# Moving 72 table stores and 8 merged-block stores of a hybrid S5 / SGU mixer layer from SyncE's DMA queue to GpSimd's

## The chip, the cores and the metric

The kernel runs on one core of one Trainium2 chip. The time is the device time of one execution in microseconds (us); lower is better. Three runs of the kernel before gave 746.2, 746.9 and 746.96 us, so its median is 746.9 us.

## The reference

One layer works on 1024 latent tokens of width 1024 and on 256 context tokens. After a layer norm and a modulation, one projection gives seven streams; two branches are computed from them, merged by sigmoid gates, projected out, and added to the input before a last layer norm.

```python
h = _layer_norm(x) * (1.0 + scale) + shift
ua, za, ub, vb, zb, ga, gb = _split_proj(h @ w_in + b_in)
y_a = s5_bidirectional(ua, state from the context)        # 32 groups of 16 channels, 64 states
ya = gelu(y_a) * sigmoid(gelu(y_a) @ glu_w + glu_b) * silu(za)
v = _layer_norm(gelu(vb)) * ln_g + ln_b
vm = einsum('gnm,bkmgc->bkngc', w_s, v in chunks of 128) + b_s
yb = gelu(ub) * vm * silu(zb)
m = sigmoid(ga) * (ya @ w_a) + sigmoid(gb) * (yb @ w_b)
x = _layer_norm(ALPHA * x + gate * (m @ w_o + b_o)) * ln_g + ln_b
```

## The kernel before

All work is float32. A product of two float32 matrices is made of three matmuls (lines 77 to 79): each weight block is loaded as `r_...`, ScalarE (ACT) rounds it to a high part `h_...` (line 72) and VectorE (DVE) subtracts to get the low part `l_...` (line 73). TensorE (PE) then multiplies high by high, low by high and high by low.

The layer norm input is transposed once, and the projection then runs block by block of 128 output channels: `blk0` to `blk3` (the u stream of the gating branch), four pieces `vb0` to `vb3` (the v stream, rows of tokens, into eight PSUM banks `pvb0` to `pvb7`, lines 691 to 699), `blk4` to `blk7` (its z stream, results `zt`), then the gates, `blk20` on. One block is 48 matmuls of 128x512. PE holds the same order of blocks throughout.

The v stream is finished in lines 700 to 708: for each of eight groups of 128 tokens DVE adds a bias out of the PSUM bank (`vt`, line 705), ACT applies gelu (line 706), DVE takes the statistics (`lv0s`, `lv0m`, lines 176 to 182), GpSimd (POOL) computes the inverse square root by a power on a 128x1 column (line 183, tile `lv0m` to `lv7m`), DVE makes the bias (line 188), ACT applies both (line 189). The chunk products `ps` of the gating unit (line 731) read all eight normalised tiles; the small product `prs` (line 719) stands ahead of them.

The state space branch is a convolution. Between about 160 and 220 us DVE makes, for four blocks b of channels and two directions, tables `kca` (lines 512 to 514), which are stored to DRAM as `cad` (line 630). PE turns them into kernels `pk` (lines 646 and 648), evacuated as `wk` (lines 652 to 657). Each `wk` is written to DRAM by eight stores `wd` (line 659), and eight DRAM-to-DRAM copies per block then expand `wd` into the Toeplitz table `mtd` (line 662). `cad` and `mtd` are read back much later (lines 780 and 783, from 400 us on). A scan over the chunk states (lines 608 to 612, three small DVE instructions a step) runs from 190 us; its first 49 steps (`scan(1, 50)`, line 682) are written ahead of the v stream.

The products of the second branch, `mb` (line 840), are stored to DRAM as `md` (line 842), one per gate block, and read back for the merge (line 896).

Every DMA goes through one helper, which issues it on SyncE (SP):

```python
    def dma(o, i):
        nc.sync.dma_start(o, i)
```

The order on each engine isn't the order of the source: a scheduler places every instruction when the program is built, from dependences, buffers and its own estimates, and each engine then works strictly down its own list. A DMA queue is such a list too. So a change of the queue can change the order on ACT, DVE and PE. Buffers come from pools by tag: `RAW` (3 buffers) holds loaded weights, `WSP` (6) their two parts, `ROW` (2) the temporaries of the tables, `G` (27) the large tiles such as `kca` and `zt`, `TMP` (4) evacuations such as `wk`. Of DMA semaphores each queue uses eight in turn, so a DMA waits until the one eight before it has landed.

Of the kernel before, what the change touches and what calls it, by code (L numbers as in the profile page):

```python
# [35 lines left out]
def mixer_kernel(ctx: ExitStack, tc: tile.TileContext, a, out):  # L36
    nc = tc.nc
# [22 lines left out]
    def BANK(name, shape=(128, 512)):  # L60
        return psum.tile(list(shape), F32, name=name, tag="b", bufs=8)

    def dma(o, i):
        nc.sync.dma_start(o, i)

    def row_bcast(name, off, n, nparts=128):
        r = a[name]
        return bass.AP(tensor=r.tensor, offset=r.offset + off, ap=[[0, nparts], [1, n]])
# [18 lines left out]
    def emit_load():  # L87
        key, ap, shape, eng = jobs[emitted[0]]
        emitted[0] += 1
        raw = RAW("r_" + key, shape)  # L90
        dma(raw, ap)
        hi, lo = WSP("h_" + key, shape), WSP("l_" + key, shape)
        split(hi, lo, raw, eng)
        loaded[key] = (hi, lo)
# [28 lines left out]

    cc = C("cc", [128, 8, 2])
    dma(cc, a["cc"])
    wmt = {}

    def load_wm(k):
        for s in range(2):
            wmt[k, s] = WSP(f"wm{k}{s}", (128, 4, 256), F32)  # L130
            dma(wmt[k, s], a["wm"][k, s])
# [362 lines left out]
    for b in range(4):  # L494
        p = BANK(f"pcu{b}")
# [6 lines left out]
    def outer(dst, tmp, eng, pr, xr, xi, b, d, last):  # L502

        gs = slice(32 * d + 8 * b, 32 * d + 8 * b + 8)
        sh = [128, 8, 8, 16]

        def bc(i, x):
            return (pr[:, :, i, gs].rearrange("p k g -> p g k").unsqueeze(3).to_broadcast(sh),
                    x[:, gs, :].unsqueeze(2).to_broadcast(sh))
        p0, x0 = bc(0, xr)  # L510
        p1, x1 = bc(1, xi)
        eng.tensor_tensor(dst, p0, x0, op=OP.mult)
        eng.tensor_tensor(tmp, p1, x1, op=OP.mult)
        eng.tensor_tensor(dst, dst, tmp, op=last)
# [105 lines left out]
    wd = dram.tile([32, 16, 240], F32, name="wd")  # L620
    mtd = dram.tile([4, 128, 8, 128], F32, name="mtd")

    cad = dram.tile([4, 2, 128, 1024], F32, name="cad")
    kca = {}

    def out_powers(b):
        for d in range(2):
            ca = G(f"kca{b}{d}", (128, 8, 8, 16))
            outer(ca, ROW("katmp", (128, 8, 8, 16)), V, pc, xcr, xci, b, d, OP.subtract)
            dma(cad[b, d], ca.rearrange("p g i h -> p (g i h)"))  # L630
            kca[b, d] = ca

    pks = {}
# [1 line left out]
    def kernels(b, d):  # L635
        if d == 0:
            pks[b] = BANK(f"pk{b}", (128, 2, 256))
        pk = pks[b]
        ca = kca[b, d]
        gg = 32 * d + 8 * b  # L640
        for k in range(4):
            for par in range(2):
                lh = bbar[:, gg + 2 * k:gg + 2 * k + 2, :].rearrange("p g h -> p (g h)")
                o = pk[32 * k:32 * k + 32, par, :]
                g = 2 * k + par
                PE.matmul(o[:, 128 * d:128 * d + 112], lh, ca[:, g, d:d + 7, :].rearrange("p i h -> p (i h)"),
                          start=True, stop=True)
                PE.matmul(o[:, 128 * d + 112:128 * d + 128], lh, xcr[:, gg + g, :], start=True, stop=True)
        if d == 0:
            return  # L650
        wk = TMP(f"wk{b}", (128, 2, 240))
        S.activation(wk[:, :, 0:112], pk[:, :, 128:240], AF.Copy)
        S.activation(wk[:, :, 128:240], pk[:, :, 0:112], AF.Copy)
        dm = TMP(f"dm{b}", (128, 3, 16))
        V.tensor_scalar(dm[:, 2, :], mask, cols[:, C_D + b:C_D + b + 1], None, op0=OP.mult)
        V.tensor_tensor(dm[:, 0:2, :], pk[:, :, 112:128], dm[:, 2, :].unsqueeze(1).to_broadcast([128, 2, 16]), op=OP.add)
        V.tensor_tensor(wk[:, :, 112:128], pk[:, :, 240:256], dm[:, 0:2, :], op=OP.add)
        for g in range(8):
            dma(wd[8 * b + g], wk[16 * g:16 * g + 16, g % 2, :])

        for s in range(8):
            dma(mtd[b, 16 * s:16 * s + 16],
                wd[8 * b:8 * b + 8, :, 16 * (7 - s):16 * (7 - s) + 128].rearrange("g h w -> h g w"))

    for i in range(2, 4):
        vm.append(G(f"vm{i}"))
    out_powers(0)
    out_powers(1)

    def kernel_step(b):  # L670
        kernels(b, 0)
        kernels(b, 1)
        if b < 2:
            out_powers(b + 2)
# [80 lines left out]
    def branch(i, g0, w, y, then, mid=None):  # L755

        banks = []

        def evac(p, sl):
            t = TMP("act")  # L760
            S.activation(t, p, AF.Sigmoid, bias=cols[:, C_BLK + g0 + i:C_BLK + g0 + i + 1])  # L761
            banks.append((t, sl))
        proj(g0 + i, evac)
        wh, wl = weights(f"{w}{i // 2}", 0 if g0 + i == GB + 7 else 2)
        if mid is not None:
            mid()
        cs_ = slice(128 * (i % 2), 128 * (i % 2) + 128)
        for t, sl in banks:
            p = BANK(f"pb{g0 + i}")
            for k in range(4):  # L770
                mm3(p, wh[:, k, cs_], wl[:, k, cs_], y[k][0][:, sl], y[k][1][:, sl], k == 0, k == 3)
            then(t, p, sl)
# [4 lines left out]
    def y_tables(b):  # L777
        for d in range(2):
            ca = WSP(f"ca{b}{d}", (128, 8, 8, 16), F32)
            dma(ca.rearrange("p g i h -> p (g i h)"), cad[b, d])  # L780
            cas[b, d] = ca
        mts[b] = RAW(f"mt{b}", (128, 8, 128))
        dma(mts[b], mtd[b])
        ums[b] = ROW(f"um{b}", (128, 8, 128))
        dma(ums[b], ud[b].rearrange("t (h g) c -> (t h) g c", g=8)[:, :, 32:160])

    def y_states(b):
        for d in range(2):
            zt = G(f"z{b}{d}", (128, 8, 128))
            o = 31 if d == 0 else 33  # L790
            for cp in range(2):
                for par in range(2):
                    dst = zt[64 * cp:64 * cp + 64, par:8:2, :]
                    src = vst[64 * par:64 * par + 64, d, o:o + 128, cp, 4 * b:4 * b + 4].rearrange("p c q -> p q c")
                    if par == 0 and cp == 0:
                        S.activation(dst, src, AF.Copy)
                    else:
                        V.tensor_copy(dst, src)
            zs[b, d] = zt
# [35 lines left out]
    md = dram.tile([8, 128, 1024], F32, name="md")  # L835
    for i in range(8):
        mb = G(f"mb{i}")

        def then_b(t, p, sl):
            V.tensor_tensor(mb[:, sl], t, p, op=OP.mult)  # L840
        branch(i, GB, "w_b", yb, then_b, mid=(lambda: y_tables(1)) if i == 7 else None)
        dma(md[i], mb)
        if i == 5:
            y_states(0)
        if i == 6:
            y_tables(0)
# [46 lines left out]
    for i in range(8):  # L893
        m.append(G(f"m{i}"))
        mb = ROW(f"mb{i}", (128, 1024))
# [14 lines left out]
        if i == 4:  # L910
# [3 lines left out]
            for h in range(2):  # L914
                p = BANK(f"pga{h}")
# [141 lines left out]
```

## Time and profile before

| | |
|---|---|
| median of three runs | 746.9 us |
| profiled execution, own time | 750.07 us |
| its span | 748.3 us |
| PE busy | 712.7 us, 95% of the span |
| PE weight loads | 588.0 us, 79% |
| DVE busy | 473.3 us, 63% |
| ACT busy | 237.3 us, 32% |
| POOL busy | 38.3 us, 5% |
| mean granted PE clock | 0.989 of full speed |

The span reaches from the first to the last instruction; the 1.77 us between it and the execution's own time lie around it. DMA issues aren't counted as busy time of an engine; they appear as rows of its queue (SPq, POOLq). Times in the rows are counted from the start of the span. "Idle before" names what ended an engine's idle time.

### The profile page before, as it was taken

Reading aid. Unit: us, or ns where it says so; the run is one execution under the profiler, and the core shown is the slowest. Engines: PE = TensorE matmul, PEld = TensorE weight load, DVE = VectorE, ACT = ScalarE, POOL = GpSimd, SP = SyncE. Lnnn points to the kernel's source line nnn. Section 1 sums busy time; section 2 is a strip of 40 time slices with the busy share of each in tenths; the row PEclk is TensorE's granted clock in tenths of the full one; section 3 lists DMA queues with packets and bytes.
Section 4 is the critical chain, followed back from the end, with each engine's and each line's share of the span. In section 5 each row is a group of like instructions: output and inputs, shape, how many; then the busy total and the mean of one; then the engine's idle time right before and its main releaser. Section 6 shows DMA issues by size and latency. Waiting matters only on the chain.

```text
span 748.3 us, 10063 instructions
## 1 busy us (share of the span) xinstructions
PE 712.7 (95%) x3924; PEld 588.0 (79%) x3924; DVE 473.3 (63%) x1067; ACT 237.3 (32%) x342; POOL 38.3 (5%) x41
## 2 busy tenths in 40 slices
PE   3899999999999699999999999999999999999995
PEld 1656888888887488888888888888888878888885
DVE  4486963559889375898989364223643334492995
ACT  3356846742103613221212265134221211350000
POOL 1010133000001100000000000000000000000221
PEclk9998999999999899999999999999999999999999
DMA  7850273624451211221212493110454223151441
GB/s 307 319 224 29 57 187 116 204 77 155 133 159 44 84 58 56 85 85 57 85 58 84 145 316 130 57 56 29 127 191 132 85 85 112 58 176 50 148 146 72
DMA packets 41295, 89.37 MB, mean 119 GB/s; under 512 B 8352, under 2 KB 21280, under 8 KB 41248
## 3 DMA queue, kind: packets, MB, share of 16 engines
q1 hardware_dynamic: 41248, 88.73, 35.3%
q8 instruction: 31, 0.51, 0.3%
q14 instruction: 16, 0.13, 0.1%
HBM read 73.02 MB, written 17.79 MB: 121 GB/s over the span
## 4 chain that ended last, share of the span: by engine, by line
PE 83%; DVE 10%; ACT 3%; DMA 2%; issue 2%; POOL 1%; SPq 0%; DVEq 0%; POOLq 0%
PE pp L77 13%; PE pp L78 13%; PE pp L79 13%; PE po L952 4%; PE po L951 4%; PE po L953 4%; PE pb L77 4%; PE pb L78 4%; PE pb L79 4%; PE pv L546 2%; DVE scm L608 2%; DVE scs L611 1%; PE py L809 1%; PE pu L77 1%; DVE vst L612 1%
## 5 line engine op out<-in xcount | busy, mean ns | idle before, releaser
L77 PE MATMUL pp<-hh,h_blk 128*128 128x512 f32 x448 | 176.5, 394 | 8.5 <-ACT h_blk L72 6.6
L78 PE MATMUL pp<-hh,l_blk 128*128 128x512 f32 x448 | 175.3, 391 | 0.0
L79 PE MATMUL pp<-hl,h_blk 128*128 128x512 f32 x448 | 174.9, 390 | 0.0
L77 PEld LDWEIGHTS pp<-hh,h_blk 128*128 128x128 f32 x448 | 84.6, 189 | 27.7 <-ACT h_blk L72 7.0
L78 PEld LDWEIGHTS pp<-hh,l_blk 128*128 128x128 f32 x448 | 84.5, 189 | 18.2 <-DVE l_blk L73 0.8
L79 PEld LDWEIGHTS pp<-hl,h_blk 128*128 128x128 f32 x448 | 84.5, 189 | 17.7
L73 DVE TENSOR_TENSOR l_blk<-r_blk,h_blk 128x1024 fp32r<-128x1024 f32 x28 | 34.9, 1248 | 54.3 <-ACT h_blk L72 54.2
L72 ACT ACTIVATE h_blk<-r_blk 128x1024 fp32r<-128x1024 f32 x28 | 29.8, 1068 | 83.1 <-PE pp L78 44.9
L761 ACT ACTIVATE act<-pp,cols 128x512 f32<-128x512 f32 x32 | 21.7, 679 | 100.0 <-PE pp L79 71.6
L608 DVE TENSOR_TENSOR scm<-acat,vst 128x128 f32<-128x128 f32 x158 | 46.1, 292 | 10.1 <-ACT vst L548 5.0
L612 DVE TENSOR_TENSOR vst<-vst,scs 128x64 f32<-128x64 f32 x158 | 35.5, 225 | 5.2
L611 DVE TENSOR_TENSOR scs<-scm 128x64 f32<-128x64 f32 x158 | 35.5, 225 | 4.9
L951 PE MATMUL po<-wobig,mh 128*128 128x512 f32 (+1 forms) x90 | 32.9, 365 | 0.0
L952 PE MATMUL po<-wobig,mh 128*128 128x512 f32 (+1 forms) x90 | 32.9, 365 | 0.0
L953 PE MATMUL po<-wobig,ml 128*128 128x512 f32 (+1 forms) x90 | 32.9, 365 | 0.0
L77 PE MATMUL pu<-hh,uw 128*128 128x512 f32 x64 | 28.5, 451 | 2.5 <-ACT uw L72 1.9
L79 PE MATMUL pu<-hl,uw 128*128 128x512 f32 x64 | 27.0, 424 | 0.9 <-DVE hl L200 0.9
L78 PE MATMUL pu<-hh,uw 128*128 128x512 f32 x64 | 26.9, 421 | 0.0
L698 PE MATMUL pvb<-l_vb,hh 128*128 128x512 f32 x64 | 25.0, 391 | 0.0
L697 PE MATMUL pvb<-h_vb,hh 128*128 128x512 f32 x64 | 25.0, 391 | 0.0
L699 PE MATMUL pvb<-h_vb,hl 128*128 128x512 f32 x64 | 24.9, 389 | 0.0
L79 PE MATMUL pb<-yas,h_w_a 128*128 128x512 f32 x64 | 24.9, 389 | 0.0
(342 smaller groups left out, 1326.7 us busy)
## 6 DMA issues: line engine op xcount, KB each, us to landing
r_blk<-in_w_blk SPq DMA_DIRECT2D x28, 512.0 KB, 3.4
wm<-in_wm SPq DMA_DIRECT2D x16, 512.0 KB, 7.3
x<-in_x SPq DMA_DIRECT2D x8, 512.0 KB, 5.8
cad<-kca SPq DMA_DIRECT2D x8, 512.0 KB, 2.7
md<-mb SPq DMA_DIRECT2D x8, 512.0 KB, 2.6
ca<-cad SPq DMA_DIRECT2D x8, 512.0 KB, 5.6
mb<-md SPq DMA_DIRECT2D x8, 512.0 KB, 4.5
wgt<-in_w_gate SPq DMA_DIRECT2D x8, 512.0 KB, 3.3
```

Of the source, the lines that this page charges most:

```text
L72: first = S.activation(hi, src, AF.Copy)
L73: return first, (eng or V).tensor_tensor(lo, src, hi.bitcast(F32), op=OP.subtract)
L77: PE.matmul(o, wh, rh, start=first, stop=False)
L78: PE.matmul(o, wl, rh, start=False, stop=False)
L79: PE.matmul(o, wh, rl, start=False, stop=last)
L608: V.tensor_tensor(scm, acat.rearrange("p d (o c) q -> p d o (c q)", o=2), both(n - 1, prev).unsqueeze(2).to_broadcast([128, 2, 2, 32]), op ...
L611: V.tensor_tensor(scs4, m4[:, :, 0, :], m4[:, :, 1, :], op=OP.add)
L612: V.tensor_tensor(both(n, 160 if n == 31 else cur), both(n, cur), scs2, op=OP.add)
L697: PE.matmul(pvb[kk], hth[k][:, ks], wh[:, j, :], start=k == 0, stop=False)
L951: PE.matmul(p, mh, wh, start=k == 0, stop=False)
L952: PE.matmul(p, mh, wl, start=False, stop=False)
L953: PE.matmul(p, ml, wh, start=False, stop=k == 7)
```

## The change

A second helper issues on GpSimd, and four kinds of DMA use it: the 8 stores `cad`, the 32 stores `wd`, the 32 expansions `mtd` and the 8 stores `md`. The helper adds four lines above everything that follows, so line 72 of the kernel before is line 76 after, and so on.

```diff
     def dma(o, i):
         nc.sync.dma_start(o, i)
+
+    def dma_side(o, i):
+
+        nc.gpsimd.dma_start(o, i)
...
             outer(ca, ROW("katmp", (128, 8, 8, 16)), V, pc, xcr, xci, b, d, OP.subtract)
-            dma(cad[b, d], ca.rearrange("p g i h -> p (g i h)"))
+            dma_side(cad[b, d], ca.rearrange("p g i h -> p (g i h)"))
...
         for g in range(8):
-            dma(wd[8 * b + g], wk[16 * g:16 * g + 16, g % 2, :])
+            dma_side(wd[8 * b + g], wk[16 * g:16 * g + 16, g % 2, :])
 
         for s in range(8):
-            dma(mtd[b, 16 * s:16 * s + 16],
+            dma_side(mtd[b, 16 * s:16 * s + 16],
                 wd[8 * b:8 * b + 8, :, 16 * (7 - s):16 * (7 - s) + 128].rearrange("g h w -> h g w"))
...
         branch(i, GB, "w_b", yb, then_b, mid=(lambda: y_tables(1)) if i == 7 else None)
-        dma(md[i], mb)
+        dma_side(md[i], mb)
```

The list of POOL in the changed program, from the last of the kernels' stores to the first block store (`lv` are the columns of the v stream's norm):

```order
L68 DMA cad_1577<-kca31_1824 128x1024
L68 DMA mtd_1576<-wd_1575 128x1x128 x8
L68 DMA wd_1575<-wk2_1889 16x240 x8
L68 DMA wd_1575<-wk3_1945 16x240 x4
L68 DMA mtd_1576<-wd_1575 128x1x128 x8
L68 DMA wd_1575<-wk3_1945 16x240 x4
L187 TENSOR_TENSOR lv0m_2348<-lv0m_2348,half_89 128x1
L187 TENSOR_TENSOR lv1m_2358<-lv1m_2358,half_89 128x1
```

```order
L187 TENSOR_TENSOR lv6m_2411<-lv6m_2411,half_89 128x1
L68 DMA mtd_1576<-wd_1575 128x1x128 x8
L187 TENSOR_TENSOR lv7m_2421<-lv7m_2421,half_89 128x1
L68 DMA md_3125<-mb0_3126 128x1024
```

In the program before, the eight `lv` columns follow directly on POOL's table arithmetic. Now 64 DMA issues stand between that arithmetic and `lv0m` (8 `cad`, 32 `wd`, 24 `mtd`), 60 of them from the first `wd` on, and 8 more between `lv6m` and `lv7m`.

The list of ACT before, around the split of weight block `blk5` (`h_blk5`); `vt` and `lv` belong to the v stream, `zt0` is the result of `blk4`:

```order
L189 ACTIVATE vt6_2406<-vt6_2406,lv6m_2411 128x512
L706 ACT_TABLE_LOAD
L706 ACTIVATE vt6_2406<-vt6_2406 128x512
L568 ACT_TABLE_LOAD
L568 ACTIVATE zt0_2427<-pp41_2460,cols_65 128x512
L72 ACTIVATE h_blk5_2291<-r_blk5_2289 128x1024
```

The same place in the changed program:

```order
L76 ACTIVATE h_vb3_2183<-r_vb3_2181 128x1024
L76 ACTIVATE h_blk4_2237<-r_blk4_2235 128x1024
L76 ACTIVATE h_blk5_2291<-r_blk5_2289 128x1024
L710 ACTIVATE vt0_2343<-vt0_2343 128x512 x2
L710 ACTIVATE vt2_2364<-vt2_2364 128x512 x2
L710 ACTIVATE vt4_2385<-vt4_2385 128x512
L76 ACTIVATE h_blk6_2430<-r_blk6_2428 128x1024
```

`h_blk5` stood twenty places behind `h_blk4`: eight gelus and seven norms of the v stream, two results `zt0` and three table loads lay between them; now it stands directly behind `h_blk4`, ahead of all of these. On DVE the biases `vt` and the statistics are likewise interleaved with the last 12 of the 49 scan steps, where they stood behind all of them. PE's list is the same but for one matmul of `blk5`, which moves 23 places back within its block.

## Rows read from the trace of the kernel before

**Rows 1.** The page: busy time by engine; the chain that ended last, by engine.
```profile
PE 712.7 (95%) x3924; PEld 588.0 (79%) x3924; DVE 473.3 (63%) x1067; ACT 237.3 (32%) x342; POOL 38.3 (5%) x41
...
PE 83%; DVE 10%; ACT 3%; DMA 2%; issue 2%; POOL 1%; SPq 0%; DVEq 0%; POOLq 0%
```

**Rows 2.** Timeline of PE, 232 to 258 us: start, us, instruction, [idle before <-releaser].
```profile
233.03 0.39 PE L699 MATMUL pvb<-h_vb,hl 128*128 128x512 f32 x1
235.26 0.47 PE L77 MATMUL pp<-hh,h_blk 128*128 128x512 f32 x1 [1.84 <-DVE vt L705]
...
253.01 1.22 PE L77 MATMUL pp<-hh,h_blk 128*128 128x512 f32 x2 [6.61 <-ACT h_blk L72]
...
257.75 0.39 PE L77 MATMUL pp<-hh,h_blk 128*128 128x512 f32 x1
```

**Rows 3.** Busy time by engine in two stretches; PEclk is the granted clock.
```profile
core 0: us, PE busy (x) PEld busy (x) DVE busy (x) ACT busy (x) POOL busy (x), PEclk, DMA share, GB/s
235.26:246.40 11.14, 11.14 (x48) 8.90 (x48) 10.16 (x34) 9.46 (x14) 3.79 (x7) 1.00 0.01 1
253.01:257.75 4.74, 4.70 (x11) 3.29 (x11) 3.57 (x3) 2.55 (x3) 0.00 (x0) 0.52 0.43 123
```

**Rows 4.** Timeline of ACT, 239 to 253 us.
```profile
239.38 0.80 ACT L189 ACTIVATE vt<-vt,lv0m 128x512 f32<-128x512 f32 x1
...
248.09 1.28 ACT L706 ACT_TABLE_LOAD   x1
...
250.03 1.28 ACT L568 ACT_TABLE_LOAD   x1
...
251.91 1.05 ACT L72 ACTIVATE h_blk<-r_blk 128x1024 fp32r<-128x1024 f32 x1
252.86 0.81 ACT L189 ACTIVATE vt<-vt,lv7m 128x512 f32<-128x512 f32 x1
```

**Rows 5.** Timeline of DVE, 185 to 236 us.
```profile
185.73 1.23 DVE L512 TENSOR_TENSOR kca<-pwf,xc 128x1024 f32<-128x1024 f32 x1 [0.28 <-PE pk L646]
...
188.14 1.22 DVE L514 TENSOR_TENSOR kca<-kca,katmp 128x1024 f32<-128x1024 f32 x1
...
234.43 1.88 DVE L705 TENSOR_TENSOR vt<-pvb,row 128x512 f32<-128x512 f32 x3
```

**Rows 6.** Timeline of SP's DMA queue, 174 to 222 us: start, us, issues.
```profile
174.94 4.93 SPq L64 DMA_DIRECT2D wd<-wk  x8
179.97 0.37 SPq L64 DMA_DIRECT2D cad<-kca  x1
...
181.16 5.13 SPq L64 DMA_DIRECT2D mtd<-wd  x8
...
219.42 1.53 SPq L64 DMA_DIRECT2D r_blk<-in_w_blk  x3
```

**Rows 7.** Timeline of POOL, 115 to 252 us.
```profile
115.40 2.03 POOL L513 TENSOR_TENSOR abtmp<-pb,yb 128x1024 f32<-128x1024 f32 x1 [6.64 <-DMA ud<-uct]
...
238.29 0.55 POOL L183 TENSOR_TENSOR lv0m<-lv0m,half 128x1 f32<-128x1 f32 x1 [106.02 <-DVE lv0m L182]
...
245.35 0.55 POOL L183 TENSOR_TENSOR lv5m<-lv5m,half 128x1 f32<-128x1 f32 x1 [0.34 <-DVE lv6m L181]
245.87 0.55 POOL L183 TENSOR_TENSOR lv6m<-lv6m,half 128x1 f32<-128x1 f32 x1
```

**Rows 8.** DMA issues by line: count, KB each, median us from issue to landing.
```profile
r_blk<-in_w_blk SPq DMA_DIRECT2D x28, 512.0 KB, 3.4
cad<-kca SPq DMA_DIRECT2D x8, 512.0 KB, 2.7
...
mtd<-wd SPq DMA_DIRECT2D x32, 64.0 KB, 2.5
...
wd<-wk SPq DMA_DIRECT2D x32, 15.0 KB, 1.5
```

**Rows 9.** Timeline of PE at 191 us and at 266 us.
```profile
191.09 0.38 PE L646 MATMUL pk<-kca,bbar 128*32 128x112 f32 x2
...
266.50 1.09 PE L719 MATMUL prs<-wst,ones 128*64 128x128 f32 x16
267.43 7.16 PE L731 MATMUL ps<-wst,vt 128*64 128x128 f32 x128
```

**Rows 10.** Timeline of PE, 439 to 448 us.
```profile
439.58 0.46 PE L809 MATMUL py<-ca,z 128*128 128x128 f32 x2 [0.48 <-DMA ca<-cad]
440.86 0.46 PE L809 MATMUL py<-ca,z 128*128 128x128 f32 x2 [0.82 <-DMA ca<-cad]
...
447.36 0.46 PE L807 MATMUL py<-mt,um 128*128 128x128 f32 x2 [0.47 <-DMA um<-ud]
```

## Prediction

> **What bounds the kernel now.** I read the page first: PE is busy for 712.7 of 748.3 us, and the chain that ended last runs through PE for 83%; POOL is busy for 38.3 us only [rows 1]. A change of the stores' queue can therefore gain only where PE waits, and lose only where it makes PE wait longer. So I read PE's timeline through the stretch in which the moved transfers are issued (175 to 270 us) and followed each gap to its releaser. There are two [rows 2]. At 235.26 PE comes out of a gap of 1.84 us: it wants a PSUM bank that DVE empties with `vt`. At 253.01 it comes out of one of 6.61 us: it wants `h_blk5`, the rounded weights of `blk5`. Then the clock. In the stretch 235.26 to 246.40 the granted clock is 1.00, the upper of its two levels, and 48 matmuls take 11.14 us, 0.232 each; from 253.01 to 257.75, behind the gap, it is 0.52, near the lower level, and the ten pitches in it take 4.74 us [rows 3]. At full clock they would take 2.32, so the dip costs 2.42. Together the place costs 1.84 + 6.61 + 2.42 = **10.9 us**.
>
> Why are these two late? DVE's first `vt` is at 234.43 [rows 5], although the last matmul of `pvb` was over at 233.42 [rows 2]: the `vt` stand behind the whole scan in DVE's list. `h_blk5` starts at 251.91, directly behind two table loads of 1.28 us each, at 248.09 and 250.03, and the instructions that need them [rows 4]. Its load wasn't late: the loads issued at 219.42 [rows 6] land 3.4 us later [rows 8], at 222.8, 29 us ahead of the split. It is the order on ACT, not the queue, that holds it.
>
> **The change, part by part.**
>
> *The new order.* In the changed program `h_blk5` stands directly behind `h_blk4`, ahead of the gelus, and the `vt` are mixed with the last twelve scan steps. Both gaps lose their releaser, and the dip behind them its cause: **−10.9 us**. What is late next is the v stream's end, because its norm needs POOL (below). From 260 us on PE's list is the same but for a matmul of `blk5`, and the waits there are under a microsecond each [rows 10], so nothing is known that would take a gain back.
>
> *The issues leave SP.* SP spends 4.93 us on eight `wd`, 5.13 on eight `mtd` and 0.37 on a `cad` [rows 6]. The transfers stay, so only these issue times leave. I cost this at nothing: PE's waits in the stretch aren't for DMAs, and the loads that stood behind the stores get ahead of their need by more than they had.
>
> *The issues come to POOL.* This decides. The inverse square roots of the v stream, `lv0m` to `lv7m`, sit on POOL, 0.55 us each, 0.52 from one to the next [rows 7]. Before, POOL was idle for 106 us ahead of `lv0m` [rows 7]. Now 60 issues stand between the first `wd`, which can start at 174.94 [rows 6] as it did on SP, and `lv0m`; eight more `mtd` stand between `lv6m` and `lv7m`. Behind POOL wait, in this order, DVE (the bias of each norm), ACT (the norm, in order with its weight splits) and PE (`ps`, which reads all eight). Call the mean time of an issue on POOL x. From the power to the norm's start it took 239.38 − 238.29 = 1.09 us [rows 4, 7], the norm takes 0.81 [rows 4]. For waits on landings among the issues I allow 2 us: SP's queue shows 181.16 − 180.34 = 0.82 between a `cad` and the `mtd` behind it [rows 6], and a `wd` lands after 1.5 [rows 8]. So the last norm is done at 174.94 + 2 + 60x + 7 × 0.52 + 8x + 1.09 + 0.81 = 182.5 + 68x.
>
> When does PE need it? Without the gaps `blk4` starts at 233.42; two blocks of 11.14 [rows 3], `prs` 267.43 − 266.50 = 0.93, and 14 of the 128 pitches of `ps` (7.16 / 128 × 14 = 0.78) until the first that reads the last tile [rows 9] give 257.4. So the cover holds for x up to (257.4 − 182.5) / 68 = **1.10 us**; each 0.1 beyond costs 6.8.
>
> The trace of before has no issue on POOL. Bounds: not under SP's own 0.62, 0.64 and 0.37 for the same transfers [rows 6], as no row has any queue issue them faster; not over 2.03, a POOL instruction over 128x1024 elements [rows 7], or 2.5, the time of a whole `mtd` to its landing [rows 8]. Between them I take what stands nearest, the shortest POOL instruction (0.55) and SP's issue together: 1.17 for a `wd`, 1.19 for an `mtd`, 0.92 for a `cad`. That counts the arithmetic of the power as well, so x is somewhat less: **1.1**, just under cover. **Stall: 0.** By the upper end, 2.5, the last norm would be done at 352.5, 95 us late; by the lower, 0.62, at 224.7 with no effect.
>
> The Trainium skill, "DMA: Bandwidth & Descriptors", section "Latency and other measured facts", gives GpSimd's queue about 1 us to the first byte against about 0.6 on the hardware path, and puts the difference down to the issue by software. Taking its 1 us for x as an estimate, the last norm is done at 250.5, under cover, and the sum is the same −10.9; no row here shows POOL's figure, while SP's 0.62 agrees with the other.
>
> *A later landing.* DVE's `kca31` started at 185.73 [rows 5]; now it waits until `cad20` has landed, because that still reads the buffer: 174.94 + 9x + 2.7 [rows 8], which is 187.5 at x = 1.1, 1.8 later. Its last instruction ended at 189.36 [rows 5], 1.73 ahead of PE's `pk` at 191.09 [rows 9]. Cost **+0.1 us** at 1.1, 3.7 at 1.5 (then covered by the greater wait).
>
> *`md`, and the tables read back.* The eight `md` come long after the norms, when POOL has nothing that others wait for. `cad` and `mtd` are read from 400 us on, over 100 us after even a slow queue. Both: 0. The two waits at 439.58 and 440.86 are for reads of `cad`, the one at 447.36 for a read of `um`, 0.48, 0.82 and 0.47 [rows 10]; if fewer entries in SP's queue removed them, 1.8 more would be gained. I take 0, and keep it for the range.
>
> **Sum:** −10.9 + 0.1 = −10.8. The profiled execution took 750.07, 3.2 over the median of 746.9 of the three runs. In its frame 739.3; against the median **736**.
>
> **Rivals.** A measurement of this kernel can tell about 0.2%, 1.5 us, from no change.
>
> *B, slower: POOL's queue becomes the bound.* If an issue takes POOL longer than 1.10, `ps` waits 68 us for each us of it, and the clock falls again behind the gap (2.42). The gain is eaten where 68(x − 1.10) + 2.4 = 10.8, at **x = 1.22**. At 1.5 the last norm is done at 284.5, 27.1 late: −10.8 + 27.1 + 2.4 = +18.7, **765.6**; at 2.03 the delay is 63.1 and the time 802. For it: nothing on POOL in this trace ends under 0.55, a full-width instruction takes 2.03, and the margin is 0.12 over my estimate. Against: the pieces I can add are already more than an issue should contain.
>
> *C, no change that can be measured.* The diff alone shifts issues from one list to another, and if the order on ACT were no help, because `h_blk5` then waits for its weights instead, the gap would stay: 746.9. Against it: those weights were issued at 219.42 and landed at 222.8 [rows 6, 8]. A band of x from 1.20 to 1.25, where gain and stall balance, belongs here too.
>
> By the Trainium skill, same page, section "Issuing engines are not separate DMA queues", all queues end on the same 16 DMA engines and a second issuer saves only its issue time, usually little; by that alone the time would be C's 746.9. The rows agree that the transfers weren't what PE waited for; the gain forecast here comes from the order of instructions, of which the rule doesn't speak.
>
> **How the numbers follow.** x decides. Under 1.10 (full gain) I give 0.43, 1.10 to 1.20 (a part of it) 0.16: faster 0.59. C with its band 0.08. B, beyond 1.25, 0.33. The likeliest is A: 736. Its own range is 734 (the three small waits go as well) to 745. B begins where A ends and is open upwards, so the range for all must reach into it: to **764**, x = 1.48, with some 0.15 above that and 0.05 below **734**.
>
> **What would show it.** Right: in PE's timeline no gap after the last `pvb` matmul and none before `blk5`, granted clock 1.00 through both blocks; POOL's queue rows of eight `wd` or `mtd` at 8.8 us or less; `lv0m` no later than 245, `lv7m` by 255.5; no gap ahead of `ps`. Wrong: issue rows of POOL over 9.8 us for eight, a gap of several us that ends with ACT's norm of `lv7m` ahead of `ps`, and a low clock behind it; or a gap at `blk5` that now ends with its load. A PE wait at `pk` near 191 us that ends with DVE would show the `kca31` term larger than 0.1.

## The result, and the profile after

The changed kernel takes **737.6 us** (median of 4 runs, 737.06 to 737.87) where the kernel before, beside it, took 746.9 (4 runs, 746.2 to 747.66). The ratio is 0.9874, 95% interval 0.9857 to 0.9891: 9.3 us, or 1.3%, faster. The forecast was 736, range 734 to 764.

The page of the changed kernel, busy time by engine, which answers to [rows 1]. Unlike issues on SP, the 80 DMA issues count among POOL's instructions (121 against 41) and as its busy time:

```profile
PE 706.3 (96%) x3924; PEld 585.1 (79%) x3924; DVE 469.7 (64%) x1067; ACT 235.1 (32%) x340; POOL 79.6 (11%) x121
```

PE's timeline from the end of the v stream to `ps`, which answers to [rows 2]; the three pieces are the start of `blk4`, the start of `blk5` and the end of both:

```profile
230.07 0.39 PE L703 MATMUL pvb<-h_vb,hl 128*128 128x512 f32 x1
230.30 0.39 PE L81 MATMUL pp<-hh,h_blk 128*128 128x512 f32 x1
...
240.95 0.39 PE L83 MATMUL pp<-hl,h_blk 128*128 128x512 f32 x1
241.18 0.39 PE L81 MATMUL pp<-hh,h_blk 128*128 128x512 f32 x1
...
252.15 1.09 PE L723 MATMUL prs<-wst,ones 128*64 128x128 f32 x16
253.07 1.37 PE L735 MATMUL ps<-wst,vt 128*64 128x128 f32 x22
```

No row carries an "idle before" any more: both gaps are gone, and `ps` starts 0.92 behind `prs`. The clock of this stretch, which answers to [rows 3]:

```profile
230.30:252.15 21.85, 21.85 (x98) 17.83 (x96) 12.65 (x51) 13.42 (x19) 7.46 (x14) 1.00 0.24 72
```

PE is busy for all 21.85 us, at granted clock 1.00, the upper level. ACT's timeline shows why:

```profile
219.39 1.06 ACT L76 ACTIVATE h_blk<-r_blk 128x1024 fp32r<-128x1024 f32 x1 [9.82 <-PE pvb L702]
...
246.82 0.69 ACT L572 ACTIVATE zt<-pp,cols 128x512 f32<-128x512 f32 x1 [0.74 <-PE pp L83]
247.50 0.82 ACT L193 ACTIVATE vt<-vt,lv7m 128x512 f32<-128x512 f32 x1
```

`h_blk5` is made at 219.39, 21.8 us ahead of `blk5`, where it stood at 251.91 [rows 4]; the last norm is done at 248.32, ahead of the point at 253.84 (253.07 + 0.77) at which `ps` first reads it. POOL's timeline, with the waits among its issues, answers to [rows 6, 7]:

```profile
172.49 3.85 POOL L68 DMA_DIRECT2D wd<-wk  x8 [1.07 <-DVE wk L661]
...
178.24 4.21 POOL L68 DMA_DIRECT2D mtd<-wd  x8 [1.34 <-issue]
...
209.07 2.03 POOL L68 DMA_DIRECT2D wd<-wk  x4
227.66 0.56 POOL L187 TENSOR_TENSOR lv0m<-lv0m,half 128x1 f32<-128x1 f32 x1 [16.55 <-DVE lv1m L185]
...
237.17 4.24 POOL L68 DMA_DIRECT2D mtd<-wd  x8
241.37 0.63 POOL L187 TENSOR_TENSOR lv7m<-lv7m,half 128x1 f32<-128x1 f32 x1
```

Eight `wd` take 3.85 us and eight `mtd` 4.21, against SP's 4.93 and 5.13 [rows 6]. POOL is through with these 60 issues (the first is at 172.49) at 211.1 and then idle for 16.55 us until DVE has statistics.

Where did the 9.3 us come from? The two profiled executions differ ahead of the change too: the first matmul of `pk` starts at 167.72 before and at 164.76 after (over all kernels of this study it lies between 162.57 and 168.02, whatever the change). This is about the 3.2 us by which before's profile stood over its median. So I compare lengths of stages, from the start of `pk` on:

| stage, us | before | after | difference |
|---|---|---|---|
| start of `pk` to start of `prs` | 98.78 | 87.39 | −11.39 |
| start of `prs` to the first `py` | 160.47 | 160.46 | 0 |
| first `py` to the last matmul's end | 313.79 | 313.39 | −0.40 |
| last output store issued to the span's end | 4.12 | 6.69 | +2.57 |

These add up to −9.2, within 0.1 of the medians' difference. The last line was not in the forecast. The rows behind it, SP's timeline at the end of the span, before (span 748.3):

```profile
744.18 0.99 SPq L64 DMA_DIRECT2D out<-r  x2
```

and after (span 736.1):

```profile
729.41 0.99 SPq L64 DMA_DIRECT2D out<-r  x2
```

The row holds the last two output stores; the stretch counts from its start. The work ahead of it is the same in both. I call this stretch **the end** below, and the first line of the table **the stage**.

### The profile page after: what moved, and what is told of

Its sections match the earlier page's. It is cut to its first block, busy times and chain, and to the rows that moved or that the text cites. A ratio compares the mean times of both kernels' runs of the same rounds, so it can differ in the third digit from the quotient of the medians.

```text
span 736.1 us, 10107 instructions
## 1 busy us (share of the span) xinstructions
PE 706.3 (96%) x3924; PEld 585.1 (79%) x3924; DVE 469.7 (64%) x1067; ACT 235.1 (32%) x340; POOL 79.6 (11%) x121
## 4 chain that ended last, share of the span: by engine, by line
PE 90%; DVE 4%; DMA 2%; ACT 2%; issue 1%; SPq 0%; POOL 0%; DVEq 0%; POOLq 0%
PE pp L81 14%; PE pp L82 14%; PE pp L83 14%; PE po L957 4%; PE po L955 4%; PE po L956 4%; PE pb L82 4%; PE pb L81 4%; PE pb L83 4%; PE pv L550 3%; PE pvb L701 2%; PE pvb L702 2%; PE pvb L703 2%; PE py L813 1%; PE pu L81 1%; PE pm L210 1%
## 5 line engine op out<-in xcount | busy, mean ns | idle before, releaser
L765 ACT ACTIVATE act<-pp,cols 128x512 f32<-128x512 f32 x32 | 21.8, 682 | 100.5 <-PE pp L83 76.5
L187 POOL TENSOR_TENSOR lo0m<-lo0m,half 128x1 f32<-128x1 f32 x1 | 1.5, 1533 | 266.7 <-DVE lo0m L186 266.7
L81 PE MATMUL pu<-hh,uw 128*128 128x512 f32 x64 | 27.4, 433 | 2.5 <-ACT uw L76 1.9
L82 PE MATMUL pu<-hh,uw 128*128 128x512 f32 x64 | 26.2, 409 | 0.0
```

The source lines that it names most:

```text
L81: PE.matmul(o, wh, rh, start=first, stop=False)
L82: PE.matmul(o, wl, rh, start=False, stop=False)
```

## Experiments

All twelve, with the medians of their own runs; the kernel before gave 746.45 beside e1 to e4, 746.91 beside e5 to e8, 747.73 beside e9 to e12. So kernels of different groups are compared by their ratios, or by stage and end, which come from their profiled executions.

| kernel | us | ratio to before (95%) | stage | end | DMAs on GpSimd |
|---|---|---|---|---|---|
| the changed kernel | 737.6 | 0.9874 (0.9857 to 0.9891) | 87.39 | 6.69 | 80 |
| e1_order_on_sp | 735.55 | 0.9853 (0.9839 to 0.9866) | 87.38 | 4.14 | 0 |
| e2_h_blk5_late | 743.67 | 0.9966 (0.9954 to 0.9979) | 94.10 | 6.47 | 80 |
| e3_one_store | 747.44 | 1.0016 (1.0005 to 1.0027) | 98.25 | 4.29 | 1 |
| e4_act_queue | 755.24 | 1.0114 (1.01 to 1.0128) | 107.35 | 4.11 | 0 |
| e5_md_only | 746.65 | 0.9999 (0.9982 to 1.0016) | 99.42 | 4.0 | 8 |
| e6_tables_only | 737.32 | 0.9867 (0.9849 to 0.9885) | 87.39 | 6.07 | 72 |
| e7_48_more | 747.65 | 1.0009 (0.9996 to 1.0023) | 87.39 | 10.6 | 128 |
| e8_96_more | 757.0 | 1.0132 (1.0116 to 1.0148) | 87.39 | 4.67 | 176 |
| e9_48_more_dve | 741.34 | 0.9914 (0.9895 to 0.9933) | 87.39 | 10.58 | 128 |
| e10_act_order_only | 738.8 | 0.9878 (0.9858 to 0.9899) | 91.12 | 4.11 | 0 |
| e11_mtd_only | 735.78 | 0.9851 (0.9826 to 0.9875) | 87.39 | 4.0 | 32 |
| e12_change_again | 737.79 | 0.9873 (0.9849 to 0.9897) | 87.39 | 6.7 | 80 |

### Is it the order or the queue? e1, e2

**e1_order_on_sp** is the kernel before with every store on SP. Edges that order instructions on one engine, without a wait, impose the changed kernel's order (`heads` holds the instructions: g gelu, n norm, z `zt`, v `vt`, s scan step).

```diff
+    def behind(later, earlier):
+        tc.add_manual_dep(later.ins, earlier.ins.name, mybir.DependencyInfo(
+            mybir.DependencyClass.NoSync, mybir.DependencyReason.DATA), reason="order")
...
+    row = "blk4 blk5 g0 g1 g2 g3 g4 blk6 g5 g6 g7 z40 n0 n1 n2 n3 n4 n5 n6 z4512 blk7 z50 n7 z5512".split()
+    row2 = [("v1", "s41"), ("v3", "s42"), ("v5", "s44"), ("v6", "s45"), ("v7", "s46")]
+    for e, l in list(zip(row, row[1:])) + row2:
+        behind(heads[l], heads[e])
```

> All stores stay on SP as in the kernel before; only the order is taken from the changed kernel: on ACT h_blk5 stands directly behind h_blk4 and the gelus, norms and zt results follow in the changed kernel's order, on DVE the eight vt stand among the scan steps 40 to 46. Theory (the order is the whole gain, the queue has no part in it): the two gaps and the dip go, 10.9 us, and the 2.6 us that the changed kernel's end became longer (from the last output store to the end of the span 6.7 us against 4.1) do not come: 735 to 736 us, 1.5 to 2.5 under the changed kernel's 737.6. Rival (SP's queue is relieved of its stores, so that loads come earlier): nothing is relieved here, 745 to 748 us, with a gap before blk5 that ends with its load.

Measured 735.55, as the theory had it. SP's timeline and ACT's:

```profile
211.61 5.05 SPq L64 DMA_DIRECT2D mtd<-wd  x8
216.70 1.53 SPq L64 DMA_DIRECT2D r_blk<-in_w_blk  x3
```
```profile
221.16 1.06 ACT L78 ACTIVATE h_blk<-r_blk 128x1024 fp32r<-128x1024 f32 x1 [11.64 <-DVE scs L617]
```

The loads of `blk5` and its followers still stand behind the last `mtd`, `h_blk5` is 1.8 us later than in the changed kernel, and it makes no difference: the stage is 87.38 long. The queue has no part in this stage's gain; the order is all of it. The 2 us by which e1 is under the changed kernel are the end: 4.14 against 6.69.

**e2_h_blk5_late** is the changed kernel with one edge more, `h_blk5` behind the second half of `zt0`:

```diff
+            if blk == ZB and sl.start:
+                behind(heads["blk5"], ev)
```

> The changed kernel with its stores on GpSimd, but h_blk5 is held behind zt0's second half on ACT, as it stood before the change. Theory (order): the gap before blk5 and the clock dip behind it come back in good part, 3 to 7 us of gap and 1 to 2.5 us of dip: 742 to 747 us; the gap of 1.84 us at blk4 stays away. Rival (relief of SP's queue): 737 to 738.5 us, no gap of over 1 us before blk5.

Measured 743.67, within the theory's range. ACT's and PE's timelines, and the clock behind the gap:

```profile
243.58 0.67 ACT L578 ACTIVATE zt<-pp,cols 128x512 f32<-128x512 f32 x1
244.15 2.94 ACT L82 ACTIVATE h_blk<-r_blk 128x1024 fp32r<-128x1024 f32 x3
```
```profile
245.24 1.22 PE L87 MATMUL pp<-hh,h_blk 128*128 128x512 f32 x2 [4.64 <-ACT h_blk L82]
```
```profile
245.24:250.00 4.76, 4.72 (x13) 3.36 (x14) 3.48 (x3) 1.84 (x2) 0.00 (x0) 0.65 0.52 151
```

With SP as relieved as in the changed kernel, the gap before `blk5` is back (4.64 us), its releaser is ACT's `h_blk` again, and the clock behind it is 0.65. The stage is 6.71 longer than in the changed kernel. The relief of SP does not help where the order is not there.

### The two gaps apart: e10

**e10_act_order_only** has e1's list `row` for ACT and not `row2` for DVE.

> All stores on SP; only ACT's order is taken from the changed kernel, on DVE the vt stay behind the whole scan. Theory (two separate terms): the gap at blk5 and the dip go (9.0 us), the gap of 1.84 us at blk4 stays: 736.9 to 738.2 us, 1.4 to 2.5 over e1_order_on_sp. Rival (the vt on DVE are what lets h_blk5 pay): 742 us or more.

Measured 738.8, a little over the range. PE's timeline and the clock behind the gap:

```profile
231.64 0.57 PE L83 MATMUL pp<-hh,h_blk 128*128 128x512 f32 x1 [1.85 <-DVE vt L711]
```
```profile
231.64:235.60 3.96, 3.96 (x11) 3.12 (x11) 3.96 (x8) 3.96 (x7) 0.00 (x0) 0.57 0.02 4
```

The gap at `blk4` is there to the hundredth, 1.85 against 1.84 [rows 2], but here the granted clock falls to 0.57 behind it, where it stayed at 1.00 in the kernel before [rows 3]. So the stage is 3.74 longer than e1's, where gap and the 0.16 by which matmuls overlap make 2.0; the dip costs the other 1.7 (ten pitches take 3.96 us, against 2.27 at full clock). In the traces ACT's order alone is worth 98.78 − 91.12 = 7.7 us, DVE's on top of it 3.7.

The dip doesn't need ACT's new order. It stands behind the same gap in e3 below, whose order on ACT is that of the kernel before:

```profile
232.69 0.47 PE L81 MATMUL pp<-hh,h_blk 128*128 128x512 f32 x1 [1.85 <-DVE vt L709]
```
```profile
232.69:236.87 4.18, 4.17 (x11) 3.27 (x12) 4.09 (x11) 2.93 (x6) 0.56 (x1) 0.59 0.02 4
```

In e3 it lengthens nothing, because the wait for `h_blk5` behind it is shorter by as much (5.01 us instead of 6.61). In e5, with the same gap (1.86), the clock stays at 1.00. Why it falls in one execution and not in another is not shown. Without the dip the two orders would be worth about 9.4 and 2.0 us, an estimate from 7.7 + 1.7 and 3.7 − 1.7, close to the 9.0 and 1.84 that were expected.

### Which of the stores turn the order: e5, e6, e11, e12

**e5_md_only** moves `md` alone, **e6_tables_only** all but `md`, **e11_mtd_only** the expansions alone; **e12_change_again** is the changed kernel beside e11.

```diff
-            dma(mtd[b, 16 * s:16 * s + 16],
+            dma_side(mtd[b, 16 * s:16 * s + 16],
```

> Only the eight block stores md go on GpSimd's queue; cad, wd and mtd stay on SP, and ACT's order is that of before. Theory (order): the gaps at blk4 and blk5 stay, nothing is gained. For the end (4.1 us before, 6.7 after the change, 4.3 with a single store on GpSimd): if it grows with the eight semaphores that a queue uses in turn, it is 6.4 to 6.8 us here and the time 748.5 to 749.5; if it grows with the number of stores, it is under 4.6 us and the time 746.5 to 747.5. Rival for the gain (it comes from the md stores leaving SP): under 745.

> The 72 stores and expansions of the tables on GpSimd, the eight md stay on SP; ACT's order is that of the changed kernel. Theory (order): all of the gain, 736.5 to 738.5 us, with an end of 6.4 to 6.8 us if it goes by semaphores or by number of stores. If the longer end belongs to md (late stores), it is 4.1 us and the time 735 us.

> Only the 32 expansions mtd go on GpSimd; ACT's order flips as in the changed kernel, with h_blk5 directly behind h_blk4. Theory (order; the end grows with the number of DMAs on GpSimd, nothing at 8 and 2 us at 72): the same gain ahead of the end, an end of 4.1 to 5.2 us, 735 to 736.5 us. Rival (all the stores must leave SP): 740 us or more.

> The changed kernel again, beside the others on one chip: 737 to 738.5 us, 1 to 3 over e11_mtd_only if the end goes by the number of DMAs, the same as it if not.

Measured 746.65, 737.32, 735.78 and 737.79. `md` gains nothing and costs nothing: both gaps stay (1.86 and 6.60 us on PE), the end is 4.0. The 32 expansions alone bring the whole stage down to 87.39, and with them gone `h_blk5` stands directly behind `h_blk4`, as ACT's timeline in e11 has it:

```profile
209.50 1.06 ACT L76 ACTIVATE h_blk<-r_blk 128x1024 fp32r<-128x1024 f32 x1 [9.82 <-PE pvb L702]
220.38 1.06 ACT L76 ACTIVATE h_blk<-r_blk 128x1024 fp32r<-128x1024 f32 x1 [9.82 <-PE pvb L702]
```

The last eight of them stood directly ahead of `blk5`'s load in SP's list, as e1's rows above show; that the scheduler reckoned this load late because of them is read from the order, not shown apart. e11 is 2.0 under the changed kernel on the same chip; the difference is the end, 4.0 against 6.7. Of the two forecasts for e5's end, the one by number of stores held.

### ACT as the issuer: e4

**e4_act_queue** is the change with `nc.scalar.dma_start` in the helper.

```diff
-        nc.gpsimd.dma_start(o, i)
+        nc.scalar.dma_start(o, i)
```

> The same 80 stores and expansions, issued on ACT instead of GpSimd. The order there has h_blk5 two places behind h_blk4, ahead of the gelus. Theory (order; end lengthened only by GpSimd's queue): the gap before blk5 goes and the end stays 4.1 us; against that stand 72 issues of about 0.6 us on ACT, 43 us between 165 and 230 us, with waits for landings among them, so PE may wait for h_vb2 or h_vb3: 735 us where it does not, up to 745 where it does. Rival (GpSimd's queue itself is needed): 746 us or more with the gap before blk5 as before.

Measured 755.24: ten over what the theory allowed, and yet without the rival's sign, the gap before `blk5`. ACT's timeline and PE's:

```profile
202.38 5.08 ACTq L68 DMA_DIRECT2D mtd<-wd  x8
207.51 0.36 ACT L656 ACTIVATE wk<-pk 128x224 f32<-128x224 f32 x1 [5.15 <-DMA mtd<-wd]
```
```profile
220.32 0.77 PE L701 MATMUL pvb<-h_vb,hh 128*128 128x512 f32 x1 [14.88 <-DVE vst L616]
```

A new gap of 14.88 us stands in the v stream, released by DVE, a little after ACT's evacuations have waited behind eight issues. The theory looked for a late weight split on ACT. That split comes directly behind the evacuations and is done at 209.56 (208.48 + 1.08), 10.8 us before the gap ends; DVE, busy with scan steps until then, makes the low part of these weights only at 221.07:

```profile
221.07 1.22 DVE L77 TENSOR_TENSOR l_vb<-r_vb,h_vb 128x1024 fp32r<-128x1024 f32 x1
```

So what came last came from DVE; why it was late there is not shown. The end is 4.11: it is GpSimd's queue that lengthens it, not the leaving of SP.

### How much POOL can carry: e7, e9, e8

**e7_48_more** and **e8_96_more** add expansions of the last table into a tile `mtx` that nothing reads, ahead of `lv0m`, and hold ACT's order by e1's list; the last two biases of the norms are also held ahead of `blk7`'s split on DVE. The diff shows e7; e8 has 12 in place of 6.

```diff
+        for j in range(6 if b == 3 else 0):
+            for s in range(8):
+                heads["extra"] = nc.gpsimd.dma_start(
+                    mtx[j, 16 * s:16 * s + 16],
+                    wd[24:32, :, 16 * (7 - s):16 * (7 - s) + 128].rearrange("g h w -> h g w"))
```

> The changed kernel with 48 more expansions of the last table on GpSimd's queue (into a DRAM tile that nothing reads), all ahead of lv0m, and the changed kernel's order held on ACT. At 0.53 us an issue they take 25 us: lv0m moves from 227.7 to about 242 us, lv7m to about 246, the last norm still before 249; PE needs it at about 254. Theory (POOL's queue has cover until then): no gap ahead of ps, 737 to 739 us. Rival (issues on POOL cost others time directly, by the DMA engines or by waits behind them): 741 us or more.

Measured 747.65: a miss. ACT's timeline and PE's:

```profile
257.59 0.81 ACT L201 ACTIVATE vt<-vt,lv0m 128x512 f32<-128x512 f32 x1 [14.95 <-DVE lv1m L200]
```
```profile
258.46 0.44 PE L752 MATMUL ps<-wst,vt 128*64 128x128 f32 x4 [2.20 <-ACT vt L201]
```

POOL had `lv0m` at 245.62, but on DVE the biases stood behind four instructions that wait for `prs`:

```profile
256.30 1.13 DVE L742 SCALAR_TENSOR_TENSOR row<-prs,cols,row 128x128 f32<-128x128 f32 x4 [11.60 <-PE prs L740]
```

The scheduler presumably put them there because it counted POOL late; that is not shown. From `prs` to `py` it took 166.43 us, 6.0 more than the changed kernel's 160.46, and the end is 3.9 longer: together the 10 us. **e9_48_more_dve** adds one edge against that:

```diff
+    behind(heads["sg0"], heads["b7"])
```

> As e7_48_more, but on DVE the eight biases of the norms stand ahead of the four instructions that wait for prs; in e7 they stood behind them, which held the norms until 257.6 us whatever POOL did. Theory (POOL's queue has cover until about 254 us): no gap of over 0.5 us ahead of ps; with the end of e7 (10.6 us against the changed kernel's 6.7), if that goes by the number of DMAs, 740.5 to 742.5 us. Rival (the queue costs time even under cover): a gap of 2 us or more ahead of ps and 745 us or more.

Measured 741.34. POOL's, ACT's and PE's timelines:

```profile
242.45 0.74 POOL L193 TENSOR_TENSOR lv0m<-lv0m,half 128x1 f32<-128x1 f32 x1
...
246.10 0.66 POOL L193 TENSOR_TENSOR lv7m<-lv7m,half 128x1 f32<-128x1 f32 x1
```
```profile
250.52 0.81 ACT L201 ACTIVATE vt<-vt,lv7m 128x512 f32<-128x512 f32 x1
```
```profile
252.91 1.26 PE L753 MATMUL ps<-wst,vt 128*64 128x128 f32 x20
```

`lv0m` is 14.8 us later than in the changed kernel and nobody waits: from `prs` to `py` 160.55. All that e9 costs is its end, 10.58.

In the expectation of **e8_96_more**, "the same" is e7:

> The same with 96 more expansions, 50 us of issues: lv0m at about 267 us, the last norm at 272 to 276, PE needs it at about 254. Theory (past its cover POOL's queue is the bound, as in the slower case of the prediction): a gap of 18 to 23 us ahead of ps that ends with ACT's norm, a low clock behind it worth about 2.4 us: 756 to 763 us. Rival (the norms are not what PE waits for): under 745 us.

Measured 757.0. POOL's timeline, PE's, and the clock behind the gap:

```profile
249.44 20.77 POOL L679 DMA_DIRECT2D mtx<-wd  x40 [2.33 <-issue]
269.92 0.87 POOL L193 TENSOR_TENSOR lv0m<-lv0m,half 128x1 f32<-128x1 f32 x1
```
```profile
271.94 9.32 PE L752 MATMUL ps<-wst,vt 128*64 128x128 f32 x95 [18.25 <-ACT vt L201]
```
```profile
271.94:281.00 9.06, 9.01 (x95) 7.42 (x97) 3.65 (x10) 8.50 (x12) 2.42 (x5) 0.62 0.13 36
```

Past its cover POOL's queue is the bound, by the chain that the prediction's slower rival named: POOL, DVE, ACT's norm, `ps`, and a low clock behind it. From `prs` to `py` it took 182.86, 22.4 more than in the changed kernel: the gap of 18.25 and 4.1 behind it.

### The end: e3

**e3_one_store** moves the first `cad` alone.

```diff
-            dma(cad[b, d], ca.rearrange("p g i h -> p (g i h)"))
+            (dma_side if (b, d) == (0, 0) else dma)(cad[b, d], ca.rearrange("p g i h -> p (g i h)"))
```

> The kernel before with one store alone, the first cad at about 168 us, on GpSimd's queue; the order on ACT is that of before. Theory (the mere use of GpSimd's queue lengthens the end of the program): the stretch from the issue of the last output store to the end of the span is 6.5 to 7 us instead of 4.1, the gaps at blk4 and blk5 stay: 749 to 750 us. Rival (the longer end comes from how many or how late GpSimd's stores are): 746 to 747.5 us, end 4.1 us.

Measured 747.44, and the end 4.29: the theory that the mere use of the queue lengthens the end falls. The 1 us by which its median lies over before's is not explained by its trace, whose stage is 0.5 shorter than before's and whose end is 0.17 longer. The DMA engines' busy tenths over the last 7 us of the span, changed kernel:

```profile
DMA  0000003999999940000000000000000000000000
```

and the kernel before:

```profile
DMA  0000000000000000000006999999910000000000
```

In the changed kernel the last transfer is over after 15 of 40 slices, and the rest, 4.4 us against some 1.6 before, shows no transfer and no counted instruction on any engine. An uncounted one stands there in the trace: a DRAIN on GpSimd. It starts with POOL's last power, 1.9 us ahead of the last output stores, and the closing steps of all engines follow when it is over. Before it runs from 742.29 for 1.01 us; in the changed kernel from 727.52 for 7.58 us, to 735.10, and the span ends at 736.1. Over all kernels it goes by the number of DMAs on GpSimd:

| DMAs on GpSimd | 0 | 1 | 8 | 32 | 72 | 80 | 128 | 176 |
|---|---|---|---|---|---|---|---|---|
| DRAIN, us | 1.01 to 1.09 | 1.11 | 1.69 | 3.66 | 6.93 | 7.58 | 11.50 | 5.53 |
| end, us | 4.11 to 4.14 | 4.29 | 4.0 | 4.0 | 6.07 | 6.47 to 6.7 | 10.6 | 4.67 |

Up to 128 that is 0.08 us for each DMA, for the 512 KB stores of e5 as for the 64 KB copies of e11 ((7.58 − 1.01) / 80 and (11.50 − 1.01) / 128 both give 0.082), long after the transfers have landed. The end grows only when the DRAIN outlasts the landing of the last stores. By these numbers that begins near 48 DMAs (an estimate: a DRAIN of 1.9 + 4.1 − 1.0 = 5.0 us). That is why e3, e5 and e11 have the end of the kernel before. At 176 the DRAIN is as long as after 55 DMAs; e8's POOL paused for 2.33 us directly behind its 128th issue (the row at 249.44 above). What GpSimd does for each DMA in the DRAIN, and in that pause, is not shown.

## Why the prediction was right, and where it was off

**What bounds the kernel, and the new order: right.** The two gaps and the dip were forecast to go for −10.9. The stage lost 11.39. Each gap is larger by the 0.16 with which matmuls overlap in the rows (0.39 long, 0.23 apart), 0.3 for both; `blk5` itself got 2.52 shorter (13.49 from its first matmul to `prs` before, 10.97 after) instead of 2.42, and `blk4` 0.1. e1 and e2 show that the order is the cause, from both sides.

Two readings behind the sum were looser than it. Not all of the 2.42 is clock: behind the gap PE's weight loads wait for `l_blk5` too, which DVE makes from the late `h_blk5`. The kernel before, PE's weight loads:

```profile
254.27 0.29 PEld L78 LDWEIGHTS pp<-hh,l_blk 128*128 128x128 f32 x1 [0.76 <-DVE l_blk L73]
```

That is about 0.6 of the 2.42, an estimate: the first three pitches take 1.85 us there (253.01 to 254.86), and 1.28 in e10 at the low clock. The new order removes this wait with the gap, so the sum holds. And e10 and e3 show that a gap of 1.85 us can bring a dip that the trace of the kernel before doesn't have.

**The issues leave SP, costed at nothing: right.** e1 keeps them all on SP and has the same stage. To that extent the Trainium skill's rule, "DMA: Bandwidth & Descriptors", section "Issuing engines are not separate DMA queues", agrees with the runs. By the rule alone the time would have stayed, as in rival C; it did not, because the change of queue came with another order.

**The issues come to POOL: right in sign, the size of the term was off.** The step "I take what stands nearest ... 1.1" took about twice the measured cost. POOL's groups by line, 165 to 245 us:

```profile
L68 POOL DMA_DIRECT2D mtd<-wd x32 | 16.9, 564 | 5.1 <-DMA wd<-wk 3.8 <-issue 1.3
L68 POOL DMA_DIRECT2D wd<-wk x32 | 15.7, 525 | 3.0 <-DMA cad<-kca 1.9 <-DVE wk L661 1.1
L68 POOL DMA_DIRECT2D cad<-kca x6 | 3.4, 562 | 7.2 <-DVE kca L518 4.0 <-DVE dm L660 1.9 <-DMA wd<-wk 1.3
```

An issue takes 0.53 to 0.56 us, below SP's 0.62 and 0.64 for `wd` and `mtd`, which the prediction had set as the lower bound: no row showed a faster queue, and that is no reason why there should be none. The allowance of 2 us for waits was too small, too: the three groups show 15.3 us of idle time, some 8 of it behind the first `wd`. Together the 60 issues took 38.6 us with their waits (172.49 to 211.10), where the prediction had 2 + 60 × 1.1 = 68. By the formula with 0.55 the last norm would be done at 219.9; it was done at 248.3, because the v stream's own statistics and the order on ACT set it, and 5.5 us ahead of its need. The mechanism was as described: e9 shows the cover and e8 its end. The Trainium skill's 1 us to the first byte on this queue, section "Latency and other measured facts" of the same page, was taken as an estimate for an issue. The rows show about half of it for POOL, and they decide; the time of an issue and the time to the first byte are also two different things, so SP's 0.62 doesn't confirm the page's 0.6 either.

**A later landing, +0.1: it was 0.** DVE's timeline:

```profile
182.77 1.23 DVE L516 TENSOR_TENSOR kca<-pwf,xc 128x1024 f32<-128x1024 f32 x1 [0.27 <-PE pk L650]
```

Against the start of `pk` this is where it stood before (185.73 − 167.72 = 18.01, and 182.77 − 164.76 = 18.01).

**`md` and the tables read back, 0: right** for `md` (e5). The waits near `py` came to 0.20 and 1.45 us (before 0.48, 0.82 and 0.47 [rows 10]), 0.1 less in all; what the rest of that stage's 0.40 is, no row here shows:

```profile
425.12 0.46 PE L813 MATMUL py<-ca,z 128*128 128x128 f32 x2 [0.20 <-DMA ca<-cad]
...
432.59 0.46 PE L811 MATMUL py<-mt,um 128*128 128x128 f32 x2 [1.45 <-DMA um<-ud]
```

**What the sum left out: the end, +2.57.** The step "Sum: −10.9 + 0.1" ends with PE's last matmul; that GpSimd's queue could cost something behind the last output was no term of it. This is why 737.6 stands where 736 was forecast, and it is what e1 and e11 win back. That the miss is only 1.6 is luck in part: the stage and the tables' reads gained about 1 us more than forecast and hid as much of it.

**The chances.** Case A held, by a wider margin than the prediction saw: it had x at 1.1 with the cover ending at 1.10, and x was half of that. Rival B's mechanism is real, but decides only far off: e9 carried 48 issues more without a wait, e8 with 96 more did not.

## What to carry to other kernels

Before a change of a DMA's queue is priced, compare the order of the instructions on the engines that PE waits for: here one weight split, moved ahead of the v stream, was worth more than everything the queues did, and the gain can be had by imposing the order with the stores left where they were (735.55 against 737.6). An engine that takes over DMA issues should be priced by the time until its next result is needed, with the waits for landings counted. And look behind the last output store: a queue can cost there what no row of PE shows. Here that was 0.08 us for each DMA issued on GpSimd, once their sum outlasted the last stores; moving the 32 expansions alone had the whole gain and none of that cost.

## What the runs showed of the hardware that was not expected

For the two frequent kinds an issue on GpSimd's queue was shorter than one on SP's (eight `mtd` in 4.21 us against 5.13, eight `wd` in 3.85 against 4.93), for `cad` it was longer (0.53 to 0.76 us against 0.37). Landings took 0.6 to 0.7 us longer for `cad`, `md` and `wd` (3.3 against 2.7 for `cad` [rows 8]), and as long as before for `mtd` (2.5). The page of the changed kernel has it for `cad`:

```profile
cad<-kca POOLq DMA_DIRECT2D x8, 512.0 KB, 3.3
```

GpSimd's DRAIN at the end of the program took 0.08 us more for each DMA on its queue up to 128 of them (11.50 us at 128), and was back at 5.53 us at 176. And the same gap of 1.85 us on PE was followed by a granted clock of 0.57 and 0.59 in two kernels and of 1.00 in two others.
